# Stick-breaking prompt attention: turning the weights by half-step, and summing the values of two heads in one run

## The chip, the cores and the metric

The kernel runs on one core of a Trainium2 chip. The metric is the device time of one execution in microseconds (us). Five engines work side by side, each on its own list of instructions: PE (matrix products; its weight loads are listed apart as PEld), DVE (elementwise work and scans), ACT (activations and copies), POOL (elementwise work) and SP (which here starts transfers).

## The reference, cut to what matters

The reference is one layer of a decoder trunk for a prompt of 2048 tokens and eight samples of four tokens. Four groups of heads (a convolution, pooling means, stick-breaking attention, attention into a memory) are concatenated and multiplied by an output matrix. The change touches the stick-breaking attention of the prompt alone, 8 heads of 64 columns:

```
z = einsum('nqhd,nkhd->nhqk', q, k) * (SB_HEAD_DIM ** -0.5) + bias     # q: query, k: key
mask = (k_pos[None, :] < q_pos[:, None])[None, None]
log_beta = log_sigmoid(z)
log_1m = where(mask, log_sigmoid(-z), 0.0)
rc = cumsum(log_1m, axis=3, reverse=True)                              # along the keys, from the end
a = exp(where(mask, log_beta + rc - log_1m, -inf))
return einsum('nhqk,nkhd->nqhd', a, v)
```

In words: a key's weight is its own sigmoid times the product of (1 - sigmoid) over all later keys that the query may see. The product is a running one along the keys, from the diagonal backwards.

## The kernel before, in words

The attention runs over *blocks*: four head pairs hp, and in each four groups qb of 512 queries. Within a block the keys are taken in *chunks* kc of 512, from the diagonal chunk (kc = qb) back to kc = 0, so a head pair has four diagonal and six off-diagonal chunks. A chunk has four *half-steps*: head hh (2) times query pair q2 (queries 0 and 1, or 2 and 3, of the four 128-query tiles). There are 160 half-steps. For each one:

- PE multiplies the scores S, four matmuls (two query tiles, two halves of an exact split; line 1267). They are 512 keys wide, in a diagonal chunk 256 for q2 = 0.
- ACT makes two gates from S: gam (line 1271) and be (line 1272), both query tiles in one instruction.
- DVE runs the product along the keys, one scan for each query tile (line 1340, in a diagonal chunk line 1337): E from gam and the carry of the chunk before.
- POOL copies the carry cr (line 1345) and multiplies be by E, once for each query tile (line 1349). The result, in be, is the weights.

The weights have queries on the partitions, while the value sums need the keys there. So PE *turns* them: a transpose of 128 x 128 for each query tile and key tile (line 1360) into a PSUM tile AT. A turn before is one key tile r of one head with up to four query tiles, 512 columns of one bank. From there ACT copies it to at in SBUF (line 1368). In a diagonal chunk queries see only earlier keys, so DVE multiplies the triangle by a mask, tri (line 1366, 128 columns for r = 0 and 1, 256 for r = 2 and 3, the last with a block of zeros), and ACT copies what is left. Then PE sums the values into av, two matmuls for a key tile, one for each head, 512 columns wide and narrower at the diagonal (line 1378). Behind a block's last sums, DVE multiplies av by the group's gate into sbo (line 1383), which SP sends out (line 1384).

What sets the order: the function sb_prompt emits the work, and yields to the work of other parts. The half-step's scores and gates come at once; its `rest` (the scans, carry and multiply) is emitted with the scores two half-steps later (`pend`); turns and sums stand in the list `late`, with the half-step at which they are due: the turns of key tile r at base + r + 6, its sums at base + r + 8, where base is the chunk's first half-step. PE does its instructions in the order in which they are written. The order on the other engines is made by a scheduler. After the last half-step eight trailing half-steps finish what is due, and output products are put among them.

Buffers: S, AT 2 each and av 1 (all PSUM), gam 3, E 3, be 10, at 4.

Of the kernel before, what the change touches and what calls it, by code (L numbers as in the profile page):

```python
# [8 lines left out]
F32 = mybir.dt.float32  # L9
# [4 lines left out]
ALU = mybir.AluOpType  # L14
# [4 lines left out]
P = 128  # L19
# [42 lines left out]
MSTEP = 5  # L62
KT = 2
WR = 2


class Tasks:
# [21 lines left out]
def kernel(  # L89
# [69 lines left out]
    ident = con.tile([P, P], F32, name="ident")  # L159
# [1129 lines left out]
    def sb_prompt(load, loaded, sb, bps, ops, zmp, early, values_of, flags, newest):  # L1289
# [5 lines left out]
                           pattern=[[-1, P]], channel_multiplier=1)  # L1295
        ZM = zmp.tile([P, 512], F32, name="ZM", bufs=1)
        act.copy(ZM, zm)
        tri = sb.tile([P, 512], F32, name="tri", bufs=1)
        pool.memset(tri, 1.0)
        pool.affine_select(out=tri, in_=tri, compare_op=ALU.is_gt, fill=0.0, base=0, pattern=[[1, 512]],  # L1300
                           channel_multiplier=-1)
        gam = []
        for k in range(3):
            g = sb.tile([P, 2, 513], F32, name=f"gam{k}", bufs=1)
# [6 lines left out]
        def score(hp, qb, kc, hh, q2, Q, KT, carry):  # L1311
# [39 lines left out]

            return rest

        def turn(hp, qb, kc, r, hh):
            dg = kc == qb
            q0 = r if dg else 0
            nm = f"{hp}_{qb}_{kc}_{r}_{hh}"
            ap_ = bps.tile([P, 512], F32, tag="AT", name=f"AT{nm}", bufs=2)
            for qt in range(q0, 4):
                pe.transpose(ap_[:, P * qt : P * (qt + 1)], A[hp, qb, kc, hh, qt][:, P * r : P * (r + 1)], ident)  # L1360
            at = sb.tile([P, 512], F32, tag="at", name=f"at{nm}", bufs=4)
            plain = 0
            if dg:
                plain = P * (q0 + 1) if r < 2 else 512
                m = slice(P * q0, plain)
                dve.tensor_tensor(out=at[:, m], in0=ap_[:, m], in1=tri[:, : plain - P * q0], op=ALU.mult)
            if plain < 512:
                act.copy(at[:, plain:], ap_[:, plain:])  # L1368
            ats[hp, qb, kc, r, hh] = at

        def values(hp, qb, kc, r, V, gt):
            dg = kc == qb
            c = slice(P * r if dg else 0, 512)
            if dg and r == 0:
                avs[hp, qb] = bps.tile([P, 512], F32, tag="av", name=f"av{hp}_{qb}", bufs=1)
            av = avs[hp, qb]
            for hh in range(2):
                pe.matmul(av[64 * hh : 64 * hh + 64, c], lhsT=V[:, 4 * kc + r, 64 * hh : 64 * hh + 64],  # L1378
                          rhs=ats.pop((hp, qb, kc, r, hh))[:, c], start=dg and r == 0, stop=kc == 0 and r == 3,
                          tile_position=(0, 64 * hh))  # L1380
            if kc == 0 and r == 3:
                mo = sb.tile([P, 512], F32, tag="sbo", name=f"sbo{hp}_{qb}", bufs=1)
                dve.tensor_tensor(out=mo, in0=av, in1=gt, op=ALU.mult)  # L1383
                (pool if (hp, qb) == blocks[-1] else sp).dma_start(mix_rows(8 + hp, 512 * qb, 512), by_tile(mo))
                flags.add((hp, qb))
# [8 lines left out]
        for bi, (hp, qb) in enumerate(blocks):  # L1394
            if bi == 0:
                values_of(0)
            if bi + 1 < len(blocks) and blocks[bi + 1] not in loaded:
                loaded[blocks[bi + 1]] = load(*blocks[bi + 1])
            Q, KT, V = loaded[hp, qb]
            V = V[hp]  # L1400
            gt = sb.tile([P, 512], F32, tag="sgt", name=f"sgt{hp}_{qb}", bufs=1)
            sp.dma_start(gt, gsd[hp, :, 512 * qb : 512 * qb + 512])
            carry = {}
            for kc in range(qb, -1, -1):
                base = step
                for hh in range(2):
# [769 lines left out]
```

## Time and profile before

| | |
|---|---|
| runs before, median of 3 | 2352.3 us (2349.05 to 2353.74) |
| the profiled execution | 2347.2 us |
| its span in the trace | 2345.5 us |
| granted clock of PE, mean | 0.994 |
| PE busy | 2264.7 us (97%), 16000 instructions |
| PEld busy | 1761.7 us (75%) |
| DVE busy | 1685.8 us (72%) |
| ACT busy | 1134.6 us (48%) |
| POOL busy | 1296.7 us (55%) |

How to read what follows. The span goes from the first instruction to the last of one profiled execution; the time of that execution lies 1.7 us above its span. Busy times are overlaps: the engines work at once. In the rows of the timeline stand the start in us, the busy time from the first start to the last end, the engine, the line of the code, the operation with output <- inputs, the shape, and how many instructions follow one another (x8). Since an instruction can begin before the one ahead has drained, the price of a group is read from its start to the next group's start. A bracket at the end of a row is idle time of the engine ahead of it, with what ended it. The attention stage lies at about 1480 to 1940 us, with the tail of the samples' attention ahead of it and the output products behind it.

### The profile page before, as it was taken

What the parts mean: (1) busy time and instruction counts of PE and PEld (TensorE: products, weight loads), DVE (VectorE), ACT (ScalarE), POOL (GpSimd) and SP (SyncE); (2) the same over time, 40 slices, a digit from 0 to 9 for tenths busy, and PEclk for the clock granted to TensorE, in tenths of its full rate; (3) what the DMA queues carried; (4) which work ended last, traced back from release to release, by engine and by line L of the source; (5) the groups of instructions that cost most, each with busy time, mean ns of one, the idle gap of its engine ahead of it and who ended that gap; (6) DMA issues with size and microseconds to landing.
All of it is one profiled execution on the core that took longest, in us unless ns stands there. A gap on an engine that the chain in (4) does not pass through costs nothing. (4 is left out here: it accounts for less than half of the span.)

```text
span 2345.5 us, 42270 instructions
## 1 busy us (share of the span) xinstructions
PE 2264.7 (97%) x16000; PEld 1761.7 (75%) x16000; DVE 1685.8 (72%) x2372; ACT 1134.6 (48%) x1999; POOL 1296.7 (55%) x1347
## 2 busy tenths in 40 slices
PE   7999999999999999999999999899999999999997
PEld 7998888888888777777777777555555557788775
DVE  5342786969657664577787868888887866686897
ACT  5332343242442222234242324799999976453553
POOL 3554546455565556545546463688988853432333
PEclk9999999999999999999999999899999999999999
DMA  6689977878678999987877884866644207876774
GB/s 206 204 292 314 339 255 267 280 252 292 239 261 316 311 351 339 324 281 263 304 272 248 288 268 143 186 165 169 167 131 117 77 23 227 283 230 195 241 247 144
DMA packets 336869, 557.94 MB, mean 238 GB/s; under 512 B 27985, under 2 KB 212433, under 8 KB 320266
## 3 DMA queue, kind: packets, MB, share of 16 engines
q1 hardware_dynamic: 281290, 286.53, 39.9%
q0 software_dynamic: 55376, 268.72, 32.4%
q8 instruction: 126, 2.06, 0.3%
q14 instruction: 77, 0.63, 0.1%
HBM read 465.09 MB, written 90.68 MB: 237 GB/s over the span
## 5 line engine op out<-in xcount | busy, mean ns | idle before, releaser
L971 DVE STREAM_TRANSPOSE T<-kt 128x1024 f32<-128x1024 f32 x256 | 308.7, 1226 | 182.4 <-PE sSA L984 175.4
L938 POOL DMA_INDIRECT vt<-in_cache_v_dram,idv x256 | 253.2, 989 | 255.3 <-PE sO L1023 194.5
L623 DVE SCALAR_TENSOR_TENSOR cacc<-U,par,cacc 128x512 f32<-128x512 f32 x480 | 360.0, 750 | 11.0
L1349 POOL TENSOR_TENSOR be<-be,E 128x512 f32<-128x512 f32 (+3 forms) x316 | 300.4, 962 | 60.9 <-DVE E L1340 23.4
L1340 DVE TENSOR_TENSOR_SCAN E<-gam,cr,ZM 128x513 f32<-128x513 f32 x192 | 233.5, 1266 | 19.5 <-ACT gam L1271 18.3
L938 POOL DMA_INDIRECT kt<-in_cache_k_dram,idk x128 | 128.2, 1001 | 198.5 <-DVE T L971 154.4
L1360 PEld LDWEIGHTS AT<-ident,be 128*128 128x128 f32 x1082 | 116.0, 142 | 125.2 <-ACT at L1368 66.6
L1995 PE MATMUL acc<-wohi,mh 128*128 128x512 f32 (+1 forms) x480 | 192.5, 401 | 1.7 <-ACT mh L1719 1.6
L1995 PE MATMUL acc<-wolo,mh 128*128 128x512 f32 (+1 forms) x480 | 188.7, 393 | 0.7 <-DVE wolo L1630 0.7
L1995 PE MATMUL acc<-wohi,ml 128*128 128x512 f32 x448 | 177.8, 397 | 7.8 <-DVE ml L1730 7.8
L1271 ACT ACTIVATE gam<-S,nbias_bc 128x1024 f32<-128x1024 f32 (+1 forms) x158 | 173.3, 1097 | 12.4 <-PE S L1267 11.6
L1267 PE MATMUL S<-kT,Q 128*128 128x512 f32 (+1 forms) x632 | 174.2, 399 | 4.8 <-ACT be L1272 4.8
L1272 ACT ACTIVATE be<-S,bias_bc 128x1024 f32<-128x1024 f32 (+1 forms) x158 | 172.3, 1090 | 0.5 <-DMA gsd<-sg1sg 0.5
L1360 PE MATMUL AT<-ident,be 128*128 128x128 f32 x1082 | 156.7, 283 | 12.3 <-ACT at L1368 6.9
L1378 PE MATMUL av<-at,V 128*64 128x512 f32 (+3 forms) x640 | 152.9, 557 | 3.7 <-DVE sbo L1383 3.7
L1368 ACT COPY at<-AT 128x512 f32<-128x512 f32 (+2 forms) x256 | 135.9, 618 | 21.4 <-PE AT L1360 12.2
L984 PE MATMUL sSA<-T,W 128*32 128x128 f32 x4096 | 138.2, 276 | 2.0 <-DVE T L971 1.6
L984 PEld LDWEIGHTS sSA<-T,W 128*32 128x32 f32 x4096 | 104.6, 110 | 36.9 <-issue 29.3
L1730 DVE TENSOR_TENSOR ml<-mr,mh 128x512 fp32r<-128x512 f32 x108 | 93.2, 870 | 42.8 <-ACT mh L1719 42.1
L1023 PE MATMUL sO<-vt,saT 128*32 128x512 f32 x1024 | 122.2, 593 | 0.0
L1267 PEld LDWEIGHTS S<-kT,Q 128*128 128x128 f32 x632 | 105.4, 194 | 18.1 <-ACT be L1272 5.8
L1337 DVE TENSOR_TENSOR_SCAN E<-gam,ZM 128x384 f32<-128x384 f32 (+1 forms) x124 | 95.5, 814 | 32.6 <-ACT gam L1271 32.3
(584 smaller groups left out, 5998.1 us busy)
## 6 DMA issues: line engine op xcount, KB each, us to landing
Q<-qd SPq DMA_DIRECT2D x64, 256.0 KB
mr<-mixd SPq DMA_DIRECT2D x32, 512.0 KB
mr<-mixd SPq DMA_DIRECT2D x48, 256.0 KB
xtp<-in_x_prompt_dram SPq DMA_DIRECT2D x16, 512.0 KB
kT<-kd SPq DMA_DIRECT2D x64, 128.0 KB
ws<-in_w_out_dram SPq DMA_DIRECT2D x16, 512.0 KB
wsd<-ws SPq DMA_DIRECT2D x16, 512.0 KB
msd<-mr SPq DMA_DIRECT2D x32, 256.0 KB
```

The costliest lines, as they stand in the source:

```text
L623: dve.scalar_tensor_tensor(out=ps, in0=U[:, a + k : a + k + H], scalar=wd[:, k : k + 1], in1=ps, op0=ALU.mult, op1=ALU.add)
L938: pool.indirect_dma_start(out=dst, out_offset=None, in_=rows, in_offset=bass.IndirectOffsetOnAxis(ap=idx, axis=0))
L971: S["turn"] = dve.transpose(T[:, 2 * hh : 2 * hh + 2].rearrange("p s j t -> p (s j t)"), kt[:, 2 * hh : 2 * hh + 2].rearrange("p s j d -> ...
L984: pe.matmul(sSs[n][32 * g : 32 * g + 32, P * ml : P * (ml + 1)], lhsT=W[:, jj, :], rhs=T[:, :, jj, :], start=i == 0, stop=i == 3, tile_pos ...
L1267: pe.matmul(S[:, j, :w], lhsT=Q[:, x, P * (q2 + j) : P * (q2 + j + 1)], rhs=kt[:, :w], start=x == 0, stop=x == 1)
L1271: act.activation(out=ga, in_=S[:, :, :w], func=AF.Sigmoid, bias=nbias_bc[:, h : h + 1], scale=-1.0)
L1272: act.activation(out=be, in_=S[:, :, :w], func=AF.Sigmoid, bias=bias_bc[:, h : h + 1])
L1340: dve.tensor_tensor_scan(out=E[:, j][:, ::-1], data0=g_[:, j][:, ::-1], data1=ZM[:, 0:1].to_broadcast([P, 513]), initial=carry[hh, q2][:, ...
L1349: newest.append(pool.tensor_tensor(out=be[:, j, :m], in0=be[:, j, :m], in1=E[:, j, 513 - w : 513 - w + m], op=ALU.mult).ins)
L1360: pe.transpose(ap_[:, P * qt : P * (qt + 1)], A[hp, qb, kc, hh, qt][:, P * r : P * (r + 1)], ident)
L1378: pe.matmul(av[64 * hh : 64 * hh + 64, c], lhsT=V[:, 4 * kc + r, 64 * hh : 64 * hh + 64], rhs=ats.pop((hp, qb, kc, r, hh))[:, c], start=dg ...
L1995: pe.matmul(o[:rows], lhsT=m[a][:, k, :rows], rhs=W[prod, 4 * h + k][w], start=not cont and h == k == n == 0, stop=h == 1 and k == 3 and n ...
```

## The change

A turn is now one half-step (one head, two query tiles) with all its key tiles, into both AT banks: off the diagonal two banks of 512 columns (two key tiles times two query tiles each), copied by ACT. On the diagonal q2 = 0 sees key tiles 0 and 1 only: one bank of 384 columns (both query tiles at r = 0, the later one at r = 1), and q2 = 2 has a whole bank, which ACT copies, and one of 384. The banks of 384 go through the mask as a whole on DVE; tri is 384 wide, with triangles at columns 0 and 256 and ones between them. The sums of a query pair are written in one run: all key tiles, both heads, 256 columns for each matmul (128 at the diagonal).

In a chunk the query pair is now the outer loop and the head the inner one, so that both heads of a pair stand together. The turn of a half-step is due four half-steps after its scores (TURN), and the sums of a pair seven after the first of its two half-steps (TURN + SUM). be has 6 buffers for 10, at 6 for 4.

By the numbers: the transposes remain 1088; copies on ACT go from 256 to 224, masks on DVE from 128 to 64; sums go from 320 matmul calls in 160 runs to 576 in 80 (each is two records in the trace); trailing half-steps from 8 to 6. Scores, gates, scans and POOL's work remain as many, in the new order.

```
-        tri = sb.tile([P, 512], F32, name="tri", bufs=1)
+        tri = sb.tile([P, 384], F32, name="tri", bufs=1)
...
-                be = sb.tile([P, 2, 512], F32, tag="be", name=f"be{nm}", bufs=10)
+                be = sb.tile([P, 2, 512], F32, tag="be", name=f"be{nm}", bufs=BEB)
...
-        def turn(hp, qb, kc, r, hh):
+        def tiles(kc, qb, q2):
+
+            last = q2 + 2 if kc == qb else 4
+            return [[(r, [qt for qt in (q2, q2 + 1) if kc < qb or qt >= r]) for r in (n, n + 1)] for n in range(0, last, 2)]
+
+        def turn(hp, qb, kc, hh, q2):
+            nm = f"{hp}_{qb}_{kc}_{hh}_{q2}"
+            for b, two in enumerate(tiles(kc, qb, q2)):
+                ap_ = bps.tile([P, 512], F32, tag="AT", name=f"AT{nm}_{b}", bufs=2)
+                at = sb.tile([P, 512], F32, tag="at", name=f"at{nm}_{b}", bufs=ATB)
+                n = 0
+                for r, qts in two:
+                    ats[hp, qb, kc, hh, q2, r] = at[:, n : n + P * len(qts)]
+                    for qt in qts:
+                        pe.transpose(ap_[:, n : n + P], A[hp, qb, kc, hh, qt][:, P * r : P * (r + 1)], ident)
+                        n += P
+                if n < 512:
+                    dve.tensor_tensor(out=at[:, :n], in0=ap_[:, :n], in1=tri, op=ALU.mult)
+                else:
+                    act.copy(at, ap_)
+
+        def values(hp, qb, kc, q2, V, gt):
             dg = kc == qb
-            q0 = r if dg else 0
...
-            if plain < 512:
-                act.copy(at[:, plain:], ap_[:, plain:])
...
+            for r, qts in sum(tiles(kc, qb, q2), []):
+                c = slice(P * qts[0], P * (q2 + 2))
+                for hh in range(2):
+                    pe.matmul(av[64 * hh : 64 * hh + 64, c], lhsT=V[:, 4 * kc + r, 64 * hh : 64 * hh + 64],
+                              rhs=ats.pop((hp, qb, kc, hh, q2, r)), start=dg and q2 == r == 0,
+                              stop=kc == 0 and q2 == 2 and r == 3, tile_position=(0, 64 * hh))
...
-                for hh in range(2):
-                    for q2 in (0, 2):
+                for q2 in (0, 2):
+                    for hh in range(2):
...
-                for r in range(4):
-                    late.append((base + r + 6, lambda a=(hp, qb, kc, r, 0): turn(*a)))
-                    late.append((base + r + 6, lambda a=(hp, qb, kc, r, 1): turn(*a)))
-                    late.append((base + r + 8, lambda a=(hp, qb, kc, r, V, gt): values(*a)))
+                for n, q2 in ((0, 0), (2, 2)):
+                    late.append((base + n + TURN + SUM, lambda a=(hp, qb, kc, q2, V, gt): values(*a)))
+                    for hh in range(2):
+                        late.append((base + n + hh + TURN, lambda a=(hp, qb, kc, hh, q2): turn(*a)))
```

How this moves instructions is shown at one place, head pair 1, block qb = 3, where the diagonal chunk kc = 3 is followed by the off-diagonal kc = 2 and 1. Names have qb and kc first; E, S and be then have head and query pair, AT and at before have key tile and head, and after they have head, query pair and bank. The last number counts buffers.

DVE before, from the scans of the second half-step of chunk 2 (E_3_2_0_2) to the last masks of the diagonal chunk:

```order
L1340 SCALAR_TENSOR_TENSOR E_3_2_0_2_17119<-gam_14877,cr_3_3_0_2_16990,ZM 128x513 x2
L1366 TENSOR_TENSOR at_3_3_0_0_17100<-AT_3_3_0_0_17095,tri 128x128
L1366 TENSOR_TENSOR at_3_3_0_1_17108<-AT_3_3_0_1_17103,tri 128x128
L1340 SCALAR_TENSOR_TENSOR E_3_2_1_0_17154<-gam_14879,cr_3_3_1_0_17025,ZM 128x513 x2
L1383 TENSOR_TENSOR sbo_2_17128<-av_2_16774,sgt_2_16508 128x512
L1366 TENSOR_TENSOR at_3_3_1_0_17135<-AT_3_3_1_0_17131,tri 128x128
L1366 TENSOR_TENSOR at_3_3_1_1_17142<-AT_3_3_1_1_17138,tri 128x128
L1340 SCALAR_TENSOR_TENSOR E_3_2_1_2_17182<-gam_14875,cr_3_3_1_2_17057,ZM 128x513 x2
L1366 TENSOR_TENSOR at_3_3_2_0_17167<-AT_3_3_2_0_17164,tri 128x256
L1366 TENSOR_TENSOR at_3_3_2_1_17172<-AT_3_3_2_1_17169,tri 128x256
L1340 SCALAR_TENSOR_TENSOR E_3_1_0_0_17208<-gam_14877,cr_3_2_0_0_17088,ZM 128x513 x2
L1366 TENSOR_TENSOR at_3_3_3_0_17194<-AT_3_3_3_0_17192,tri 128x128
```

The last masks (key tile 3) stand behind scans of the next chunk but one. DVE after, from the first mask of the same diagonal chunk to its last:

```order
L1376 TENSOR_TENSOR at_3_3_0_0_0_17089<-AT_3_3_0_0_0_17088,tri 128x384
L1345 SCALAR_TENSOR_TENSOR E_3_2_0_0_17135<-gam_14876,cr_3_3_0_0_17014,ZM 128x513 x2
L1393 TENSOR_TENSOR sbo_2_17118<-av_2_16774,sgt_2_16540 128x512
L1376 TENSOR_TENSOR at_3_3_1_0_0_17122<-AT_3_3_1_0_0_17121,tri 128x384
L1345 SCALAR_TENSOR_TENSOR E_3_2_1_0_17164<-gam_14878,cr_3_3_1_0_17043,ZM 128x513 x2
L1345 SCALAR_TENSOR_TENSOR E_3_2_0_2_17198<-gam_14880,cr_3_3_0_2_17084,ZM 128x513
L1376 TENSOR_TENSOR at_3_3_0_2_1_17151<-AT_3_3_0_2_1_17150,tri 128x384
L1345 SCALAR_TENSOR_TENSOR E_3_2_0_2_17198<-gam_14880,cr_3_3_0_2_17084,ZM 128x513
L1345 SCALAR_TENSOR_TENSOR E_3_2_1_2_17227<-gam_14876,cr_3_3_1_2_17106,ZM 128x513 x2
L1376 TENSOR_TENSOR at_3_3_1_2_1_17184<-AT_3_3_1_2_1_17183,tri 128x384
L1345 SCALAR_TENSOR_TENSOR E_3_1_0_0_17265<-gam_14878,cr_3_2_0_0_17138,ZM 128x513 x2
```

The eight narrow masks have become four wide ones; the last one now stands behind the scans of the half-steps of chunk 2 and ahead of all scans of chunk 1.

PE before, the half-steps of chunk 1 that hold the last two key tiles of the diagonal chunk:

```order
L1267 MATMUL S_3_1_0_2_17174<-kT_1_0_16101,Q_3_0_16497 128x512 x4
L1378 MATMUL av_3_17161<-at_3_3_1_0_17135,V_15600 64x384
L1378 MATMUL av_3_17161<-at_3_3_1_1_17142,V_15600 64x384
L1360 MATMUL AT_3_3_3_0_17192<-ident,be_3_3_0_2_16924 128x128
L1360 MATMUL AT_3_3_3_1_17196<-ident,be_3_3_1_2_16984 128x128
L1267 MATMUL S_3_1_1_0_17200<-kT_1_1_16107,Q_3_1_16503 128x512 x4
L1378 MATMUL av_3_17161<-at_3_3_2_0_17167,V_15600 64x256
L1378 MATMUL av_3_17161<-at_3_3_2_1_17172,V_15600 64x256
L1360 MATMUL AT_3_2_0_0_17217<-ident,be_3_2_0_0_17019 128x128 x2
L1360 MATMUL AT_3_2_0_0_17217<-ident,be_3_2_0_2_17051 128x128 x2
```

Turns and sums of one key tile stand in every half-step. PE after, the last turns of the diagonal chunk and its first sums:

```order
L1373 MATMUL AT_3_3_1_0_0_17121<-ident,be_3_3_1_0_16973 128x128 x3
L1271 MATMUL S_3_2_0_2_17127<-kT_2_0_16287,Q_3_0_16529 128x512 x4
L1373 MATMUL AT_3_3_0_2_0_17143<-ident,be_3_3_0_2_17008 128x128 x4
L1373 MATMUL AT_3_3_0_2_1_17150<-ident,be_3_3_0_2_17008 128x128 x3
L1271 MATMUL S_3_2_1_2_17156<-kT_2_1_16293,Q_3_1_16535 128x512 x4
L1388 MATMUL av_3_17171<-at_3_3_0_0_0_17089,V_15627 64x256
L1388 MATMUL av_3_17171<-at_3_3_1_0_0_17122,V_15627 64x256
L1388 MATMUL av_3_17171<-at_3_3_0_0_0_17089,V_15627 64x128
L1388 MATMUL av_3_17171<-at_3_3_1_0_0_17122,V_15627 64x128
L1373 MATMUL AT_3_3_1_2_0_17176<-ident,be_3_3_1_2_17037 128x128 x4
L1373 MATMUL AT_3_3_1_2_1_17183<-ident,be_3_3_1_2_17037 128x128 x3
L1271 MATMUL S_3_1_0_0_17190<-kT_1_0_16146,Q_3_0_16529 128x512 x4
```

The diagonal chunk's last turn (AT_3_3_1_2_1) has moved ahead of chunk 1's first scores; the next turn on PE behind these is AT_3_2_0_0_0, and AT_3_2_0_0_1 takes the bank of AT_3_3_1_2_1. Value sums stand in every second half-step, four of them in a row here and eight for a whole query pair.

More of the change, by code (lines that the diff above doesn't have):

```diff
@@ L64 @@
 WR = 2
+TURN = 4
+SUM = 3
+BEB = 6
+ATB = 6
 class Tasks:
@@ L1297, in sb_prompt @@
         act.copy(ZM, zm)
-        tri = sb.tile([P, 512], F32, name="tri", bufs=1)
+        tri = sb.tile([P, 384], F32, name="tri", bufs=1)
         pool.memset(tri, 1.0)
-        pool.affine_select(out=tri, in_=tri, compare_op=ALU.is_gt, fill=0.0, base=0, pattern=[[1, 512]],
-                           channel_multiplier=-1)
+        for c in (0, 256):
+            pool.affine_select(out=tri[:, c : c + P], in_=tri[:, c : c + P], compare_op=ALU.is_gt, fill=0.0, base=0,
+                               pattern=[[1, P]], channel_multiplier=-1)
         gam = []
@@ L1352, in score @@
             return rest
-        def turn(hp, qb, kc, r, hh):
-            dg = kc == qb
-            q0 = r if dg else 0
[L1357 to L1366, printed above, removed]
-            if plain < 512:
-                act.copy(at[:, plain:], ap_[:, plain:])
-            ats[hp, qb, kc, r, hh] = at
@@ L1371, in values @@
[L1371 to L1374, printed above, removed]
+        def tiles(kc, qb, q2):
[16 more added lines that the diff above has]
+                    act.copy(at, ap_)
@@ L1375, in values @@
+        def values(hp, qb, kc, q2, V, gt):
+            dg = kc == qb
+            if dg and q2 == 0:
                 avs[hp, qb] = bps.tile([P, 512], F32, tag="av", name=f"av{hp}_{qb}", bufs=1)
             av = avs[hp, qb]
-            for hh in range(2):
-                pe.matmul(av[64 * hh : 64 * hh + 64, c], lhsT=V[:, 4 * kc + r, 64 * hh : 64 * hh + 64],
-                          rhs=ats.pop((hp, qb, kc, r, hh))[:, c], start=dg and r == 0, stop=kc == 0 and r == 3,
-                          tile_position=(0, 64 * hh))
@@ L1381, in values @@
-            if kc == 0 and r == 3:
+            for r, qts in sum(tiles(kc, qb, q2), []):
[4 more added lines that the diff above has]
+                              stop=kc == 0 and q2 == 2 and r == 3, tile_position=(0, 64 * hh))
+            if kc == 0 and q2:
@@ L1405, in sb_prompt @@
                 base = step
-                for hh in range(2):
-                    for q2 in (0, 2):
+                for q2 in (0, 2):
+                    for hh in range(2):
                         cost = 1.33 * (2 * q2 + 3) / 4 if kc == qb else 2.66
```

## Prediction

> **What bounds the kernel now.** I read the page first, then the busy time of the attention stage, then that stage step by step. The stage is a fifth of the span, and all five engines are loaded in it:
>
> ```profile
> span 2345.5 us, 42270 instructions
> 1480.00:1940.00 460.00, 439.51 (x2440) 259.08 (x2441) 373.59 (x486) 421.08 (x593) 372.28 (x470) 0.99 0.46 124
> ```
>
> The columns are PE, PEld, DVE, ACT and POOL, then the clock. PE is busy for 96% of it, ACT 92%, DVE 81%. Behind the stage PE goes on with the output products without a break, so a microsecond here is one at the end. A plain stretch (off-diagonal chunk after off-diagonal chunk) looks like this on PE, then on ACT:
>
> ```profile
> 1656.42 1.09 PE L1360 MATMUL AT<-ident,be 128*128 128x128 f32 x8
> 1657.27 1.17 PE L1267 MATMUL S<-kT,Q 128*128 128x512 f32 x4
> 1658.37 1.08 PE L1378 MATMUL av<-at,V 128*64 128x512 f32 x4
> 1659.38 1.09 PE L1360 MATMUL AT<-ident,be 128*128 128x128 f32 x8
> ...
> 1658.48 1.14 ACT L1271 ACTIVATE gam<-S,nbias_bc 128x1024 f32<-128x1024 f32 x1
> 1659.49 1.13 ACT L1272 ACTIVATE be<-S,bias_bc 128x1024 f32<-128x1024 f32 x1
> 1660.49 1.09 ACT L1368 COPY at<-AT 128x512 f32<-128x512 f32 x2
> 1661.44 1.16 ACT L1271 ACTIVATE gam<-S,nbias_bc 128x1024 f32<-128x1024 f32 x1
> ```
>
> From start to start: eight transposes 0.85 us, four score matmuls 1.10, a group of sums 1.01; together 2.96 on PE. ACT needs 1.01 + 1.00 + 0.95 = 2.96 as well, each instruction beginning before the one ahead has drained. Both are full. The narrower sums of the diagonal chunks, and the sO group, which is sixteen records in one run:
>
> ```profile
> 1608.47 0.87 PE L1378 MATMUL av<-at,V 128*64 128x384 f32 x4
> 1609.27 0.44 PE L1360 MATMUL AT<-ident,be 128*128 128x128 f32 x2
> ...
> 1610.57 0.65 PE L1378 MATMUL av<-at,V 128*64 128x256 f32 x4
> 1611.15 1.09 PE L1360 MATMUL AT<-ident,be 128*128 128x128 f32 x8
> ...
> 1453.69 0.39 PE L247 MATMUL z1sg<-xhi,wlo1sg 128*128 128x512 f32 x1
> 1453.93 0.60 PE L552 MATMUL mpt<-ident,pr 128*128 128x128 f32 x4
> 1454.45 1.95 PE L1023 MATMUL sO<-vt,saT 128*32 128x512 f32 x16
> 1456.34 0.19 PEld L247 LDWEIGHTS z1sg<-xhi,whi1sg 128*128 128x128 f32 x1 [0.81 <-issue]
> ```
>
> A group of sums takes 1.01, 0.80 and 0.58 us at 512, 384 and 256 columns, by the line 0.37 at 128: 0.43 per 256 columns and 0.16 that does not depend on the width. The sO run, 1.89 us, is four quads of 0.43 and 0.18, so the fixed part belongs to the run and not to the matmul.
>
> One head pair, ten chunks, lies between these rows, and PE waits in it at these places:
>
> ```profile
> 1583.15 0.72 PE L1267 MATMUL S<-kT,Q 128*128 128x256 f32 x4
> 1583.80 0.65 PE L1378 MATMUL av<-at,V 128*64 128x512 f32 x2
> ...
> 1613.12 0.44 PE L1378 MATMUL av<-at,V 128*64 128x128 f32 x4
> 1614.06 0.93 PE L1360 MATMUL AT<-ident,be 128*128 128x128 f32 x6 [0.49 <-ACT at L1368]
> 1614.74 0.72 PE L1267 MATMUL S<-kT,Q 128*128 128x256 f32 x4
> 1616.69 1.08 PE L1378 MATMUL av<-at,V 128*64 128x512 f32 x4 [1.23 <-DVE sbo L1383]
> ...
> 1642.04 0.65 PE L1378 MATMUL av<-at,V 128*64 128x256 f32 x4
> 1643.19 1.06 PE L1360 MATMUL AT<-ident,be 128*128 128x128 f32 x8 [0.51 <-DVE at L1366]
> ...
> 1674.61 0.65 PE L1378 MATMUL av<-at,V 128*64 128x256 f32 x4
> 1675.76 0.41 PE L1360 MATMUL AT<-ident,be 128*128 128x128 f32 x2 [0.50 <-DVE at L1366]
> ...
> 1690.75 0.72 PE L1267 MATMUL S<-kT,Q 128*128 128x256 f32 x4
> ```
>
> Against the prices above the waits are 0.57 + 1.30 + 0.57 + 0.57 = 3.0 us (1613.12 to 1614.06 is 0.94 for a group worth 0.37, and so on). The head pair took 1690.75 - 1583.15 = 107.6 us. I price a chunk by what PE does in its four half-steps: its own scores, and the transposes and sums of the chunk before. With o for off-diagonal and d for diagonal, and four 256-wide scores at 0.65: o after o 4 x 2.96 = 11.84; d after o 1.30 + 2.20 + 3.40 + 4.04 = 10.94; o after d 4.40 + 2.10 (20 transposes) + 2.76 = 9.26; d after d 8.36. A head pair has 3, 3, 3 and 1 of these: 104.5, and with the waits 107.5. The prices hold.
>
> **What the change saves.** The sums of a chunk now stand in two runs instead of four, so 20 runs of a head pair's 40 lose their 0.16. An o run is 0.16 + 4 x 0.43 = 1.87 us; the two d runs are 0.80 and 1.65. The added matmuls (576 calls for 320, half as wide) cost nothing inside a run, by the sO row.
>
> [...]
>
> Where scores are no longer followed by sums, they lose what they pay at the change of kind: S to av is 1.10 where four spacings of 0.23 are 0.94, and the row z to mpt (0.24) shows no such payment between a matmul of this sort and transposes. Between 0 and 0.16 for a half-step; I take 0.08 (1.02, and 0.57 for a narrow one). PE then needs: o after o 11.38, d after o 3.34 + 3.40 + 3.74 = 10.48, o after d 4.24 + 2.10 + 2.45 = 8.79, d after d 7.89. But ACT still has 11.84 in o after o, where nothing of its work is removed, and 4 x 2.01 + 2 x 0.47 = 9.0 in o after d, where one whole copy replaces two narrow ones per head. Taking the larger each time: 35.5 + 31.4 + 27.0 + 7.9 = 101.8 us a head pair, if nothing new waits.
>
> **What it costs: the mask's place on DVE.** The diagonal chunk's triangles are cut by DVE, while the copies are ACT's. Here is DVE in such a chunk now:
>
> ```profile
> 1659.72 2.46 DVE L1340 TENSOR_TENSOR_SCAN E<-gam,cr,ZM 128x513 f32<-128x513 f32 x2 [0.92 <-ACT gam L1271]
> ...
> 1666.64 2.45 DVE L1340 TENSOR_TENSOR_SCAN E<-gam,cr,ZM 128x513 f32<-128x513 f32 x2
> 1669.00 0.67 DVE L1383 TENSOR_TENSOR sbo<-av,sgt 128x512 f32<-128x512 f32 x1
> 1669.58 0.48 DVE L1366 TENSOR_TENSOR at<-AT,tri 128x128 f32<-128x128 f32 x2
> 1669.98 2.45 DVE L1340 TENSOR_TENSOR_SCAN E<-gam,cr,ZM 128x513 f32<-128x513 f32 x2
> 1672.34 0.73 DVE L1366 TENSOR_TENSOR at<-AT,tri 128x256 f32<-128x256 f32 x2
> 1672.99 2.45 DVE L1340 TENSOR_TENSOR_SCAN E<-gam,cr,ZM 128x513 f32<-128x513 f32 x2
> 1675.35 0.47 DVE L1366 TENSOR_TENSOR at<-AT,tri 128x128 f32<-128x128 f32 x2
> 1675.73 2.45 DVE L1340 TENSOR_TENSOR_SCAN E<-gam,cr,ZM 128x513 f32<-128x513 f32 x2
> ```
>
> From 1666.64 on it has no gap for 9 us: a pair of scans 2.36, sbo 0.58, two masks 0.40 at 128 columns and 0.65 at 256. The last mask ran at 1675.35 although its transposes had begun at 1673.3: the scans of 1672.99 stood ahead of it, and PE waited 0.57. Before, the masks of a step stand behind the scans of the half-step one earlier, and the last of them come two steps later than now. By the order, in the changed program the third mask stands behind half, and the fourth behind all, of the scans of the half-step in which its own transposes run. The first turn of the next chunk needs that bank for its second four transposes, since AT has two.
>
> Count from the end of the chunk's first off-diagonal scores to the second bank of the next chunk's first turn. DVE: 1.35 until the first scan (scores over at 1658.37, scan at 1659.72), four pairs of scans 9.44, three masks, sbo 0.58. A 384-column mask is in no row; between 0.33 (256) and 0.58 (sbo, 512), by the line 0.45. Sum 12.7. PE in the same stretch: transposes 0.32 + 0.32 + 0.74 + 0.74 + 0.42, scores 1.10 + 1.02 + 1.10 + 1.02, sums 1.87 + 0.80: 9.45. PE waits 3.3. The lower end is the case in which DVE has no backlog: after the last scores 1.35 + 2.36 + 0.45 against 2.98 of PE's work, 1.2. I take 3.3, since DVE is unbroken here even now. While PE waits, no scores are issued, and ACT runs dry too; nothing covers it.
>
> [...]
>
> So o after d becomes 8.79 + 3.3 = 12.1. In d after d the scans are a third shorter; the wait lies between 0 and 1.2, I take 0.6. A head pair: 35.5 + 31.4 + 36.3 + 8.5 = 111.7, against 107.6: 4.1 longer, and four of them 16 us.
>
> **Edits at nothing.** The sbo wait (1.30 and 0.57) goes, and is already out of the sum: a block's last sums and the next block's first now stand two half-steps apart. be's six buffers: a half-step's is read last four half-steps later and needed again after six. at's six: the sums that free one precede the turn that takes it. Half as many DVE masks, each longer: 4 x 0.45 against 1.43 for two heads, in the sum. The gate load on SP waits for sbo, two half-steps sooner. Two trailing half-steps less: the output matmuls that stood in them follow at once. If the cover of these fails, a half-step late costs up to 2.96 once a block.
>
> **The rivals.** *The masks are in time* (faster): the saving on PE then shows. With a wait of 1.2 a head pair is 35.5 + 31.4 + 30.0 + 8.5 = 105.4, with none 101.8: 9 to 23 us less, 2343 to 2329. For it: sums and waits go from PE for certain. Against it: DVE's unbroken rows. It decides at 1.9 us of wait (35.5 + 31.4 + 26.4 + 3 x 1.9 + 8.5 = 107.6), so DVE's 12.7 would have to be 1.4 shorter. *No change*: a wait of 1.5 to 2.3, in which gain and loss cancel; 2352. *The long runs keep the fixed part for every key tile*: an o run would be 4 x 0.58 for 1.87, so o after o 12.28, d after o 11.38, d after d 0.6 more: 4.6 a head pair, 18 us on top, 2387. Against it stands the sO row.
>
> **The numbers.** The profiled execution took 2347.2 us (span 2345.5); with 16 it would be 2363. The three runs' median, 2352.3, is 5 above it; so 2369. Chances: 0.68 for the forecast, 0.16 for masks in time, 0.11 for no change, 0.05 for the costlier runs. The range reaches down to the edge of no change, and up by the mask at 0.58 and a start of the scans half a microsecond late (0.9 a chunk, 11 us): 2347 to 2380. About 0.2%, 4.7 us, is what a measurement of this kernel can tell from none: slower 0.73, same 0.11, faster 0.16.
>
> **What would show it.** A head pair from first scores to first scores in about 112 us; PE's waits for at from DVE grown from half a microsecond to 3 us behind each diagonal chunk that an off-diagonal one follows, in front of the second bank of the first turn (some 40 us in the stage); sums in runs of 1.87 us; the wait for sbo gone; o after o still near 11.8 with ACT full. I am wrong if head pairs are below 106, or if PE's waits are on something else.

## The result and the profile after

The changed kernel takes 2380.7 us (median of 4 runs, 2376.9 to 2395.2) beside 2351.8 us of the kernel before: a ratio of 1.0128, 95% interval [1.0086, 1.0170]. Two later rounds on other chips gave 1.0113 [1.0089, 1.0137] and 1.0131 [1.0113, 1.0149]. A fifth run on record, which is not in the median, took 2375.0 us. The kernel is slower, as forecast, but by 29 us where 17 were forecast, and the median lies just above the range (the medians of the two later rounds, 2378.9 and 2383.4, lie on either side of its end). In the experiments below, one of the ten runs of e5 fell into a slow state, 3667 us at a granted clock of 0.557, and is left out of e5's figures.

The profiled execution is the longest of the four. Of the 48.0 us between its span and that before, 13.2 lie ahead of the stage, where the two programs are the same (the first scores begin at 1486.26 instead of 1473.09; in the two later traces of the same kernel at 1473.37 and 1476.23). The stage itself, from the first scores to the last sums, is 35.1 us longer. Busy time and clock of that stretch, before and then after (columns: window and length, then PE, PEld, DVE, ACT, POOL busy, the granted clock, DMA):

```profile
1473.09:1938.74 465.65, 440.99 (x2448) 259.89 (x2446) 375.09 (x489) 427.99 (x603) 374.75 (x477) 0.99 0.47 127
```

```profile
1486.26:1987.03 500.77, 437.02 (x2957) 311.87 (x2955) 376.76 (x425) 425.61 (x570) 376.25 (x478) 0.96 0.43 118
```

In the two later traces the stage has 498.1 and 499.3 us. What PE waited for in it, before and after (total, times, longest):

```profile
PE AT L1360 <- ACT at L1368: 6.9, 13, 1.9
PE S L1267 <- ACT be L1272: 4.8, 2, 3.0
PE AT L1360 <- DVE at L1366: 3.8, 7, 0.7
PE av L1378 <- DVE sbo L1383: 3.7, 3, 1.2
```

```profile
PE AT L1373 <- DVE at L1376: 36.5, 27, 2.5
PE AT L1373 <- ACT at L1378: 13.0, 23, 1.1
PE S L1271 <- ACT be L1276: 7.6, 2, 4.0
```

PE's idle time went from 465.65 - 440.99 = 24.7 us to 63.8, and five sixths of the growth is the mask. The clock has fallen from 0.99 to 0.96 as well, which the prediction did not have. Here is one place where both are seen, the first turn behind head pair 1's chunk (1, 0); first PE:

```profile
1637.34 0.63 PE L1373 MATMUL AT<-ident,be 128*128 128x128 f32 x4 [0.17 <-ACT at L1378]
1638.88 0.55 PE L1373 MATMUL AT<-ident,be 128*128 128x128 f32 x3 [0.92 <-DVE at L1376]
1639.19 0.72 PE L1271 MATMUL S<-kT,Q 128*128 128x256 f32 x4
1639.84 0.63 PE L1373 MATMUL AT<-ident,be 128*128 128x128 f32 x4
1642.87 0.73 PE L1373 MATMUL AT<-ident,be 128*128 128x128 f32 x4 [2.40 <-DVE at L1376]
1643.28 1.18 PE L1271 MATMUL S<-kT,Q 128*128 128x256 f32 x4
1644.39 2.87 PE L1388 MATMUL av<-at,V 128*64 128x256 f32 x16
1647.19 1.09 PE L1373 MATMUL AT<-ident,be 128*128 128x128 f32 x8
```

and DVE at the same time:

```profile
1634.30 0.54 DVE L1376 TENSOR_TENSOR at<-AT,tri 128x384 f32<-128x384 f32 x1
1634.76 3.62 DVE L1345 TENSOR_TENSOR_SCAN E<-gam,cr,ZM 128x513 f32<-128x513 f32 x3
1638.30 0.53 DVE L1376 TENSOR_TENSOR at<-AT,tri 128x384 f32<-128x384 f32 x1
1638.75 3.62 DVE L1345 TENSOR_TENSOR_SCAN E<-gam,cr,ZM 128x513 f32<-128x513 f32 x3
1642.28 0.53 DVE L1376 TENSOR_TENSOR at<-AT,tri 128x384 f32<-128x384 f32 x1
```

DVE has no gap. PE needs the second bank at about 1640.3 (1639.84 and four transposes); the mask that frees it was asked for at 1638.88, stands behind three scans, and runs from 1642.28 to 1642.81. PE goes on at 1642.87. The scores and sums that follow then take about 1.7 times as long: the sixteen sums from 1644.39 to 1647.19 are 2.80 us, where the same run elsewhere takes 1.66 (1669.52 to 1671.18; a run of sixteen that are all 256 wide takes 1.88). The clock of the three stretches, the wait, the time behind it, and what follows:

```profile
1639.84:1643.28 3.44, 1.04 (x10) 0.80 (x9) 3.44 (x6) 1.74 (x3) 3.18 (x3) 1.00 0.96 213
1643.28:1646.80 3.52, 3.52 (x19) 2.35 (x19) 1.43 (x3) 1.85 (x3) 3.14 (x8) 0.52 1.03 365
1646.80:1654.00 7.20, 7.20 (x56) 5.42 (x53) 2.61 (x3) 5.82 (x8) 2.48 (x4) 1.00 0.32 120
```

By the trace's record of the clock, the stage after has 8 spells at half clock (0.50 in the record), of 3.41 or 6.83 us; before it has 2, of 6.83 us, at its start. The stop above was 2.40 us, and PE was busy for 1.04 of the 3.44 us in front of the spell (first row). Half of the time in spells is 18.8 us after and 6.8 before. That is the most that they can cost, an estimate from the granted clock (the scores and sums above, in a spell of 3.41 us, took 3.91 us, where the same took 2.31 in e6, rows further down); an idle PE loses nothing, and over PE's busy time alone it is 15.8 and 5.9. So the stage's 35.1 us are: 39.1 more idle, 9.9 more lost to the clock, and 13.9 less work (437.02 - 15.8 against 440.99 - 5.9).

### The profile page after: what moved, and what is told of

Read it like the earlier page. It is cut to its first block, busy times and chain, and to the rows that moved or that the text cites. A ratio compares the mean times of both kernels' runs of the same rounds, so it can differ in the third digit from the quotient of the medians.

```text
span 2393.5 us, 43149 instructions
## 1 busy us (share of the span) xinstructions
PE 2266.5 (95%) x16512; PEld 1817.6 (76%) x16512; DVE 1686.7 (70%) x2308; ACT 1133.7 (47%) x1967; POOL 1297.7 (54%) x1348
## 3 DMA queue, kind: packets, MB, share of 16 engines
q1 hardware_dynamic: 281290, 286.53, 39.1%
## 5 line engine op out<-in xcount | busy, mean ns | idle before, releaser
L1354 POOL TENSOR_TENSOR be<-be,E 128x512 f32<-128x512 f32 (+4 forms) x316 | 301.9, 963 | 94.6 <-DVE E L1342 46.9
L1373 PE MATMUL AT<-ident,be 128*128 128x128 f32 x1082 | 159.1, 283 | 52.5 <-DVE at L1376 36.5
L1378 ACT COPY at<-AT 128x512 f32<-128x512 f32 x224 | 126.7, 626 | 33.8 <-PE AT L1373 33.2
L1388 PE MATMUL av<-at,V 128*64 128x256 f32 (+1 forms) x1152 | 142.1, 389 | 0.0
L1388 PEld LDWEIGHTS av<-at,V 128*64 128x64 f32 x1152 | 78.8, 142 | 60.0 <-issue 30.2
```

Of the source, the lines that this page charges most:

```text
L1354: newest.append(pool.tensor_tensor(out=be[:, j, :m], in0=be[:, j, :m], in1=E[:, j, 513 - w : 513 - w + m], op=ALU.mult).ins)
L1373: pe.transpose(ap_[:, n : n + P], A[hp, qb, kc, hh, qt][:, P * r : P * (r + 1)], ident)
```

## The experiments

All times are medians beside runs of the kernel before on the same chip; waits and spells are those of PE in the stage, and "lost" is half of the time in spells, the most that they can cost.

| run | us | ratio, 95% interval | stage, us | wait for DVE's mask | wait for ACT's copies of at | spells, lost us |
|---|---|---|---|---|---|---|
| before | 2351 | | 465.7 | 3.8 | 6.9 | 2, 6.8 |
| changed | 2380.7 | 1.0128 [1.0086, 1.0170] | 500.8 | 36.5 | 13.0 | 8, 18.8 |
| e1 mask ahead of the turn | 2357.7 | 1.0036 [1.0020, 1.0052] | 478.5 | none | 28.7 | 3, 8.5 |
| e2 turns two half-steps later | 2370.7 | 1.0082 [1.0052, 1.0112] | 489.3 | 27.9 | 12.3 | 6, 13.7 |
| e3 order alone, on before | 2356.1 | 1.0021 [1.0000, 1.0042] | 468.5 | 4.6 | 8.3 | 2, 8.5 |
| e4 mask ahead of the turn, on before | 2356.7 | 1.0024 [1.0003, 1.0046] | 471.3 | none | 11.7 | 3, 8.5 |
| e5 masks first on DVE | 2350.9 | 1.0007 [0.9987, 1.0027] | 468.6 | 2.5 | 24.3 | 4, 8.5 |
| e6 scores repeated | 2371.9 | 1.0092 [1.0066, 1.0118] | 490.4 | 26.5 | 13.3 | 1, 5.1 |
| e7 sums in two runs | 2377.3 | 1.0113 [1.0095, 1.0131] | 494.2 | 28.9 | 2.8 | 6, 15.4 |
| e8 = e5 and e7 | 2346.6 | 0.9978 [0.9968, 0.9988] | 466.5 | 1.9 | 7.0 | 2, 6.8 |
| e9 changed again | 2378.9 | 1.0113 [1.0089, 1.0137] | 498.1 | 35.5 | 12.8 | 7, 17.1 |
| e10 = e8, one half-step later | 2354.5 | 1.0014 [0.9998, 1.0029] | 473.2 | 2.4 | 7.0 | 3, 8.5 |
| e11 scores repeated, again | 2375.0 | 1.0099 [1.0080, 1.0117] | 491.8 | 26.6 | 13.2 | 1, 6.8 |
| e12 changed, a third time | 2383.4 | 1.0131 [1.0113, 1.0149] | 499.3 | 35.1 | 12.8 | 8, 18.8 |

**e1, the mask taken out of the way.** The two 128-column triangles are cut on be, behind the scans of the half-step itself:

```
+                if dg:
+                    for j, n in enumerate(ns):
+                        dve.tensor_tensor(out=be[:, j, n - P : n], in0=be[:, j, n - P : n], in1=tri, op=ALU.mult)
...
-                if n < 512:
-                    dve.tensor_tensor(out=at[:, :n], in0=ap_[:, :n], in1=tri, op=ALU.mult)
-                else:
-                    act.copy(at, ap_)
+                act.copy(at[:, :n], ap_[:, :n])
```

> The changed kernel, but the triangles are cut before the turn: DVE multiplies the two 128-column blocks of be by a triangle right behind the half-step's scans, in the diagonal chunk where DVE has idle time, and ACT copies all turned banks, the 384-column ones too. Theory (the late mask): the waits of PE for at from DVE (36.5 us in the stage after, 3.8 before) go to under 3 us, with them the six further spells of half clock (some 12 us); ACT's 64 narrow copies are 64 x 0.36 = 23 us more, mostly where ACT has room. The stage comes to 450 to 460 us (465.7 before, 500.8 after), the time to 2335 to 2350 us. Rival (turning into both banks at once is itself what stops PE, whoever empties the bank): the waits move to ACT's copies, 25 us or more of them, and the time stays at 2370 us or above.

2357.7 us, 7 above the kernel before on the same chip: 22 of the 29 us are gone, and so are the spells in the middle of the stage but one. But both theories missed. The theory's time was too low, since new waits came; the rival's waits for ACT's copies did come (28.7 us, where it asked for 25), but not its time of 2370. So the late mask is most of the loss. What is left is for the most part PE's waits for copies, of which the old turns, with ACT copying all as here (e4 below), have 11.7:

```profile
PE AT L1375 <- ACT at L1377: 28.7, 42, 4.3
PE AT L1375 <- POOL be L1356: 9.2, 10, 1.5
PE S L1271 <- ACT be L1276: 7.7, 2, 4.2
```

**e2, turns later.** TURN 6 for 4, BEB 8 for 6.

> The changed kernel with TURN 6 instead of 4 and 8 be buffers instead of 6: turns and sums two half-steps later, the masks where they are on DVE in relation to their transposes, but the last two of a diagonal chunk now run in the second off-diagonal chunk. Theory (the late mask by DVE's backlog: in the four half-steps behind a diagonal chunk DVE has four pairs of scans, four masks and sbo, 9.44 + 4 x 0.45 + 0.58 = 11.8 us, against 9.5 of PE): two masks and sbo leave that stretch, the waits for at from DVE fall from 36.5 to 10 to 20 us, the time to 2350 to 2368 us. Rival (the place in the queue alone: a mask behind the scans of the half-step in which it is asked for): the waits stay at 30 us or more, the time at 2375 to 2390 us.

2370.7 us, and 27.9 us of waits for the mask: between the two. Spreading the masks over more time helps by 10 us, but most of the wait is still there: a mask that is asked for two half-steps later stands behind the scans of a half-step two later.

**e3, the order alone, and e4, the mask ahead of the turn alone, on the kernel before.**

```
-                for hh in range(2):
-                    for q2 in (0, 2):
+                for q2 in (0, 2):
+                    for hh in range(2):
```

> The kernel before with one part of the change: in a chunk the query pair is the outer loop and the head the inner one; turns, masks, copies and sums as before. Theory (the late mask of the new turns): nothing of the cost comes with the order, 2345 to 2360 us, waits for at from DVE under 8 us. Rival (the order of the half-steps costs): 2365 us or more.

> The kernel before with the triangles cut on be ahead of the turn as in the first run, and all turned banks copied by ACT alone; turns, order and sums as before. Theory: the masks cost the kernel before 3.8 us of waits, and ACT gets the masks' columns on top, so 2345 to 2358 us. Rival (cutting ahead of the turn is a gain by itself, which would make the first run no evidence on the change): 2342 us or less.

2356.1 and 2356.7 us, both in the theory's range. The order of the half-steps, with the turns as before, accounts for some 5 us (by its interval 0 to 10), where the theory gave it nothing. Cutting the mask early is no gain by itself, so that e1's 22 us belong to the new turns' masks.

**e5, the place in the queue.** Nothing but DVE's order: the scans are queued behind the last mask that was written before them.

```
-                    if dg:
...
+                    with tc.issue_after(masks[-1]) if masks else ExitStack():
+                        if dg:
...
-                    dve.tensor_tensor(out=at[:, :n], in0=ap_[:, :n], in1=tri, op=ALU.mult)
+                    masks.append(dve.tensor_tensor(out=at[:, :n], in0=ap_[:, :n], in1=tri, op=ALU.mult).ins)
```

> The changed kernel with nothing but the order of DVE altered: each half-step's scans are queued behind the last mask that was written before them, so that every mask stands one pair of scans earlier. Same instructions, same PE order. Theory (the place of the masks in DVE's queue, with its backlog): the waits of PE for at from DVE fall from 36.5 us to under 12, the further spells of half clock go, what stays is PE's 16 us of saved work less 15 to 25 us of waits for ACT's copies: 2335 to 2358 us. Rival (DVE's sum of 11.8 us in the four half-steps behind a diagonal chunk binds in whatever order): the scans come late in the masks' place, PE waits for be from POOL or for scores' gates instead, 2362 us or more.

2350.9 us, which cannot be told from the kernel before. DVE behind a diagonal chunk, and PE's waits:

```profile
1667.53 2.45 DVE L1346 TENSOR_TENSOR_SCAN E<-gam,cr,ZM 128x513 f32<-128x513 f32 x2
1669.89 0.53 DVE L1377 TENSOR_TENSOR at<-AT,tri 128x384 f32<-128x384 f32 x1
1670.34 2.45 DVE L1346 TENSOR_TENSOR_SCAN E<-gam,cr,ZM 128x513 f32<-128x513 f32 x2
1672.71 0.53 DVE L1377 TENSOR_TENSOR at<-AT,tri 128x384 f32<-128x384 f32 x1
1673.15 21.35 DVE L1346 TENSOR_TENSOR_SCAN E<-gam,cr,ZM 128x513 f32<-128x513 f32 x18
```

```profile
PE AT L1374 <- ACT at L1379: 24.3, 40, 1.3
PE S L1271 <- ACT be L1276: 6.0, 2, 3.5
PE AT L1374 <- DVE at L1377: 2.5, 3, 1.0
```

The same instructions on every engine, in the same order on PE (on ACT and POOL a few have changed places), and 34 us of PE's waits for DVE are gone. The masks stand one to two pairs of scans earlier, the last one two: in the changed kernel's rows further up it runs behind eight scans of the off-diagonal chunk (two ahead of those rows, then three and three), here behind four. The scans that had to stand back are done without a gap right behind, with those that follow in one stretch of 21.35 us, and PE hardly waits for that (1.7 us for be from POOL in the stage, 1.2 in the changed kernel): the rival, that DVE's sum binds in any order, falls. What is left is 24.3 us of waits for ACT's copies, which take the place of the masks.

**e6, e11 and e12, the clock.** PE does the scores twice or three times in front of the turn that stops:

```
-                sb_scores(S, h, q2, w, Q[hh], KT[hp, hh, kc])
+                again = (hh, q2) == (0, 0) and kinds[-3:-1] == [True, False]
+                for _ in range(1 + again * (2 if dg else 1)):
+                    sb_scores(S, h, q2, w, Q[hh], KT[hp, hh, kc])
```

> The changed kernel with work added: in the first half-step of the chunk that follows an off-diagonal chunk behind a diagonal one, PE does the scores twice (three times where they are 256 wide) into the same bank, in front of the turn that waits for the late mask. 1.1 to 1.3 us of PE work at 11 places, 13 us in all. Theory (a stop of PE of 2 to 2.4 us is followed by some 4 us at half the granted clock, which costs about 1.6 us each time): the wait behind the repeated scores shrinks by what they take, the clock stays whole there, and the time falls by 3 to 10 us against the changed kernel in spite of the added work: 2368 to 2377 us. Rival (the half clock costs nothing, since DVE sets the pace there anyway): the same time or up to 13 us more, 2378 to 2394 us.

> The changed kernel with repeated scores again, this time on the same chip and in turn with the changed kernel itself. Theory (half clock behind each stop of over 2 us costs about 1.6 us): 4 to 10 us less than the changed kernel, at most one spell of half clock outside the first 60 us of the stage. Rival (the gap seen between the two in different calls was their scatter): within 3 us of it.

> The changed kernel, to stand beside the run with repeated scores: 2374 to 2383 us, five to seven spells of half clock in the stage behind its first 60 us if the two traces so far are typical.

2371.9 us in e6. In the second round, in turn with the changed kernel on one chip, 2375.0 (2368.9 to 2381.4) against 2383.4 (2381.0 to 2386.7): 8 us less time with 64 more matmuls (at 12 places, not 11); the intervals of the two ratios overlap by 0.0004, and e6 against the first result says the same. In the stage of e6 PE has 12 us more of work at full clock and waits 10 us less for the mask; what makes it 10.4 us shorter than that of the first trace is the clock, 3.1 us lost over PE's busy time for 15.8. The same place as above in e6, where the stop is 1.56 us instead of 2.40 and the sums behind it are at full speed (1629.58 to 1631.24):

```profile
1624.84 1.68 PE L1271 MATMUL S<-kT,Q 128*128 128x256 f32 x12
1626.36 0.60 PE L1375 MATMUL AT<-ident,be 128*128 128x128 f32 x4
1628.52 0.65 PE L1375 MATMUL AT<-ident,be 128*128 128x128 f32 x4 [1.56 <-DVE at L1378]
1628.93 0.71 PE L1271 MATMUL S<-kT,Q 128*128 128x256 f32 x4
1629.58 1.73 PE L1390 MATMUL av<-at,V 128*64 128x256 f32 x16
1631.24 1.09 PE L1375 MATMUL AT<-ident,be 128*128 128x128 f32 x8
```

The traces of e6 and e11 have one spell each, at the start of the stage, where the changed kernel's three have 7 or 8. So the half clock is a part of the loss by itself, and no accident of one trace.

**e7 and e8, the sums in two runs.** Key tiles 0 and 1, then 2 and 3 a half-step later; at has 8 buffers:

```
-            for r, qts in sum(tiles(kc, qb, q2), []):
+            for r, qts in tiles(kc, qb, q2)[half]:
...
+                    for half in range(len(tiles(kc, qb, q2))):
+                        late.append((base + n + TURN + SUM + half, lambda a=(hp, qb, kc, q2, V, gt, half): values(*a)))
```

> The changed kernel with one part undone: the sums of a query pair in two runs, key tiles 0 and 1, and 2 and 3 one half-step later (8 at buffers instead of 6), so that every half-step has eight sums. Theory: 64 more runs at 0.16 us are 10 us of PE work, most of it in places where PE waits for the mask or ACT anyway: 0 to 10 us more than the changed kernel, 2378 to 2392 us. Rival (the uneven half-steps, with sums only in every second one, make PE wait for ACT's copies, 13 us in the stage): the waits for ACT fall below 7 us and the time falls by 3 us or more, 2366 to 2377 us.

> Both of the above: the masks queued ahead of the scans, and the sums in two runs. Theory (late masks, and one long run saves 0.16 us a run): 0 to 10 us more than with the masks first alone. Rival (uneven half-steps cost waits for ACT's copies): 3 to 10 us less than with the masks first alone; then it is the version that could beat the kernel before.

By itself the split moves nothing: 2377.3 us, the ratio of e9, between the ranges of the theory and the rival. The waits for copies go to 2.8 us, as the rival said, but the mask still stops PE. With the masks first it does: 2346.6 us, the one version of these below the kernel before (0.9978, at most 0.9988), and its waits:

```profile
PE AT L1374 <- ACT at L1379: 7.0, 21, 0.6
PE AT L1374 <- POOL early L1355: 5.2, 2, 4.9
PE av L1389 <- DVE sbo L1394: 4.6, 4, 2.3
```

Against e5, on the same chip, that is 4.3 us less; the intervals of the two ratios just touch. Why a part that undoes PE's saving helps is seen in one head pair, of before, e5 and e8 in turn:

```profile
1583.15:1690.75 107.60, 104.88 (x595) 61.66 (x594) 91.37 (x116) 104.07 (x146) 96.84 (x121) 1.00 0.61 170
```

```profile
1587.54:1695.23 107.69, 101.13 (x723) 73.12 (x722) 90.57 (x101) 102.10 (x137) 95.14 (x120) 1.00 0.61 173
```

```profile
1592.33:1699.44 107.11, 104.61 (x723) 71.14 (x722) 90.44 (x101) 102.48 (x137) 95.44 (x121) 1.00 0.61 173
```

With its one run e5 saves 3.7 us of PE's work per head pair, but PE's half-steps then alternate (one with sixteen sums, the next with none) while ACT's are all alike, and with two banks PE cannot run ahead: the saving comes back as idle time, 6.6 us for 2.7, of which 6.0 are waits for ACT's copies. ACT is busy for 95 to 97% of the pair in each.

**e9 and e10.** The changed kernel once more, and e8 with TURN 5 and 7 be buffers.

> The changed kernel once more, for a second trace and a second time beside the kernel before. Theory: stage 497 to 503 us, seven or eight spells of half clock in it, waits for at from DVE 34 to 39 us, 2374 to 2384 us. Rival (the spells of half clock, and with them a third of the loss, were an accident of one execution, like the 13 us by which its stage began late): three spells or fewer, the stage under 492 us.

> The version with the masks first and the sums in two runs, and the turns and sums one half-step later (TURN 5, 7 be buffers). What it should take away: the 5 us in which PE waits at the start of the stage for the first weights from POOL, and slack for weights that come late from POOL. Theory: the stage's steady parts are set by ACT (2.96 us a half-step) and do not move; 0 to 5 us less than the version with TURN 4, 2340 to 2350 us. Rival (each half-step of delay brings the last masks of a chunk nearer to the backlog of the next scans): waits for at from DVE above 8 us and 2352 us or more.

e9 repeats the first trace without the late start of its stage. e10 missed: 2354.5 us. The wait at the start only moved: where PE in e8 waits 4.86 us for the first weights, in e10 it waits 4.63 at the same place of the stage for the bank of its next scores. And PE waits 9.1 us for sbo, in 11 places, where e8 has 4.6 in 4. No mask came late, so it is not the rival's reason either; why sbo comes later there was not followed up.

## Why the prediction was right in sign and too small

- **The late mask.** Right in mechanism, and nearly in size: 3.3 us forecast per diagonal chunk with an off-diagonal one behind it, 42 us in all; the stage has 36.5. It comes in two waits and not in one. Around the end of chunk (2, 1) of head pair 1 they are 0.82, ahead of the second bank of the diagonal chunk's last turn, and 2.08, ahead of the second bank of the next chunk's first turn (see below). That the queue order makes it is shown by e5, with the same instructions and the same order on PE.

```profile
1663.99 0.55 PE L1373 MATMUL AT<-ident,be 128*128 128x128 f32 x3 [0.82 <-DVE at L1376]
...
1667.98 0.66 PE L1373 MATMUL AT<-ident,be 128*128 128x128 f32 x4 [2.08 <-DVE at L1376]
...
1669.52 1.74 PE L1388 MATMUL av<-at,V 128*64 128x256 f32 x16
1671.18 0.98 PE L1373 MATMUL AT<-ident,be 128*128 128x128 f32 x7
```

- **The step that failed** is the sum of a head pair, "35.5 + 31.4 + 36.3 + 8.5 = 111.7", times four. Its 16 us are some 35 us more idle time and 19 less work on PE (a head pair 11.9 idle for 3.0, and 99.8 of work for 104.5), at full clock throughout; the stage shows 39.1 more idle, 13.9 less work, and 9.9 for the clock. Most of the miss is a term that the sum does not have, the next one a size.
- **The missing term** is the half clock behind a long wait, which the prediction put at nothing without a reason: 9.9 us more than before over PE's busy time in the stage (8.4 and 10.6 in the two later traces). e6 and e11 give back 8 to 9 us by filling the stops.
- **The size of the saving.** "PE then needs" forecast 104.5 to 99.8 us of work a head pair (3 x 11.38 + 3 x 10.48 + 3 x 8.79 + 7.89). The changed kernel has 103.95 us in head pair 1, 102.2 without its spell; e5, which has no spell there, goes from 104.88 to 101.13. The run of sixteen sums does take the 1.87 us that were worked out (1.88, rows below).
- **"Taking the larger each time"**, of PE's and ACT's work in a chunk, holds where both are even: an off-diagonal chunk after an off-diagonal one, with no mask to wait for, came to 11.92 for 11.84 (first row below). It fails where they are not: a diagonal chunk after an off-diagonal one took 11.15 for 10.48 (second row), though PE is busy for 10.54 of it and ACT for 10.46:

```profile
1712.78:1724.70 11.92, 11.65 (x83) 8.10 (x82) 9.80 (x9) 11.92 (x17) 10.91 (x12) 1.00 0.29 70
1607.89:1619.04 11.15, 10.54 (x83) 7.91 (x82) 6.53 (x9) 10.46 (x17) 7.70 (x10) 1.00 0.87 256
```

PE at the head of that diagonal chunk, and ACT:

```profile
1607.89 0.72 PE L1271 MATMUL S<-kT,Q 128*128 128x256 f32 x4
1609.21 1.06 PE L1373 MATMUL AT<-ident,be 128*128 128x128 f32 x8 [0.61 <-ACT at L1378]
...
1610.68 1.95 PE L1388 MATMUL av<-at,V 128*64 128x256 f32 x16
1612.56 1.09 PE L1373 MATMUL AT<-ident,be 128*128 128x128 f32 x8
```

```profile
1608.30 1.26 ACT L1378 COPY at<-AT 128x512 f32<-128x512 f32 x2
```

ACT comes out of the off-diagonal chunk with its copies still to do, and the next turn needs the banks that they empty: 0.6 us at the head of three of this head pair's four diagonal chunks. (The fourth, chunk (2, 2), has the mask's wait and the spell at 1643 in its place.) Such waits for ACT are 13.0 us in the stage, 6.1 more than before.
- **Head pair 1 in one line.** The sum was 111.7; it took 116.81 (116.75 in both later traces). The 5.1 between are 2.4 of PE's work, 1.7 for the spell, 1.4 of waits for ACT's copies (2.8, where taking the larger gave 1.4) and 0.5 for be from POOL, less 1.0 by which the mask was put too high (9.5 for 10.5). That last error hides a part of the others.
- **The sbo wait** went, as forecast (PE has no idle time ahead of its sums after); it came back in e7, e8 and e10, where the sums lie closer to the next block's. **The trailing half-steps**, put at nothing, gave 4 us: from the last scores to the last sums 24.35 us for 28.31. The new order of the half-steps was not priced either; alone, on the kernel before, it costs some 5 us (e3, 0 to 10). The stage's first head pair lost most, 121.6 us for 110.1, among other things by two of the new spells, which the prediction, working from head pair 1, did not look at.
- **The rivals.** The costlier runs fell by the 1.88 us. The masks in time would not have been worth the forecast 2343 to 2329: e5 has them in time, and stands at 2351, since waits for ACT's copies take the masks' place. No change needed a wait of 1.5 to 2.3 us a chunk; the waits come to 2.9 to 3.3.

What stays open: how much of the 24.3 us of waits in e5 is the alternation and how much is ACT's own fullness; e8 removes 17 of them but gives PE more work for it. e7 and e8 also have two at buffers more, which were not tried alone; in e5 all 14.6 us that ACT is idle ahead of its copies end with PE's turn, and none with the sums that free an at buffer.

## What to carry to other kernels

When a change makes one engine ask another for something small at a new moment, look at what stands ahead of that small thing in the other engine's queue: here one to two pairs of scans decided over 34 us of waits, and an ordering edge without any change of work took them away. Where two engines are both nearly full (PE was busy for 95% of the stage before, ACT for 92%), work taken from one of them in lumps can come back as waits for the other (24.3 us in e5, 7.0 with the sums spread in e8); try it with half-steps that stay alike. A wait of two microseconds on PE has to be priced with the half clock that can follow: behind the first 60 us of the stage, 14 of the 30 stops of 1.98 us or more in the changed kernel's three traces went with a spell, and a spell of 3.41 us cost up to 1.7 us.

## What the hardware showed that was not expected

In the changed kernel's three traces, leaving out the first 60 us of the stage, each of the 9 stops of PE of 2.40 us or more went with a spell of half clock, and 5 of the 21 stops between 1.98 and 2.08 us. In e6 and e11 the longest stop there is of 1.98 us, the others are of 1.6 us or less, and none went with a spell. The length alone does not decide: in e7 a stop of 2.53 us went without a spell, and in e10 one of 1.83 us with one.

The clock's record shows what went with a spell. Within one trace all spells of the stage begin on one grid of 3.41 us (the eight of the changed kernel, from 1493.13 to 1878.84, to a nanosecond), and last one step of it or a few (3.41 to 13.65 us). Cutting the stages of all 14 traces along their grids, a spell followed on each of the 42 steps at full clock in which PE was busy for less than 45% of the time, on 10 of the 25 between 45% and 52.5%, and on 4 of the 1825 above, all four in the first 60 us of a stage. So it was with the stop ahead of 1643.28, which falls into one step (PE busy for 1.04 of 3.44 us) and went with a spell; the 2.08 us that end at 1667.98 lie in two, with PE busy for 1.91 of the 3.42 us of the first and 2.64 of the 3.41 of the second, and went without one.

Since a spell of one step cost up to 1.7 us of PE's work (1.60 behind 1643.28), PE was faster for doing a piece of work twice in e6 and e11.
